# A decoder trunk on one core: pages and PSUM banks as numbered slots, bank turns in the plan, modulation loads at new places

## The chip, the cores and the metric

One core of a Trainium2 chip runs the whole program; the other cores are idle. The metric is the device time of one execution in microseconds (us), the median of three runs. All inputs lie in the chip's memory (HBM) in float32 and the result is written back there.

## The reference, cut to what matters

Two layers on 256 tokens of width 2048. Layer 0 mixes with native sparse attention (NSA: compressed, selected and windowed keys, 16 query heads on 4 key heads), layer 1 with stick-breaking attention; each has a SwiGLU channel mixer of inner width 5632. A vector c gives shift, scale and gate for every norm.

```python
for layer in range(2):
    mod = silu(c) @ mod_w[layer] + mod_b[layer]            # 2048 x 12288, float32
    sh1, sc1, g1, sh2, sc2, g2 = split(mod, 6)
    h = rms_norm(x, g0) * (1 + sc1) + sh1
    if layer == 0:
        y = nsa_mixer(h, ...)                              # w_in 2048 x 5168, w_out 2048 x 2048
    else:
        hk = rms_norm(x, kv_norm_g) * (1 + kv_sc) + kv_sh  # kv_mod_w 2048 x 4096
        k, v = split(hk @ kv_w)                            # 2048 x 4096
        y = stick_breaking(h @ w_q, k, v) @ w_out
    x = x + g1 * rms_norm(y, g1n)
    h = rms_norm(x, g2) * (1 + sc2) + sh2
    gate, up = split(h @ ffn_w_in[layer])                  # 2048 x 11264
    x = x + g2 * rms_norm((silu(gate) * up) @ ffn_w_out[layer], g3)
```

## The kernel before, in words

**Matmuls.** A weight matrix is cut into blocks of 512 rows by 512 columns (1 MB). Each block is fetched into a page of SBUF (a tile of 128 x 2048, 23 pages in all) named raw, and split into two float32r pages: ScalarE copies it rounded (wh), VectorE subtracts (wl = raw - wh). The activations are split the same way. A block meets a half of the tokens (t = 0 or 1) in 12 matmuls of 128x512: high x high, high x low, low x high for four k slices. The results gather in a PSUM bank (acc). Eight banks are shared by these accumulators ("mm") and by all other uses ("x": transposes, scores). In layer 1's channel mixer ("F1") eight of the eleven inner blocks go through a Strassen scheme ("st" units, tiles sacc, rawX, rawY, rawZ, rawW, Sh, Sl, yp), merged between the other units.

**Modulation.** The vectors come from float32 pages of mod_w: 16 loads (modw) for each vector, each followed by one VectorE multiply-add (macc) over 128 x 2048. The first two vectors go by quarters through TensorE (modq, qacc).

**The plan.** The program is written out in full by a planner, `Emit`, while the kernel is built: it keeps a clock for each engine (`clk`), a price for each instruction (`_cost`), and decides from them in which order instructions are put on the engines' queues. `units` is the fixed order of matmul groups on TensorE. `run_bg` advances the epilogues (generators that `yield` until a time). `pump` decides when a block is split and when the next load is put on SP's DMA queue: `LEADS`, `URGENT`, `target` (how many split blocks may wait), `reserve` and `raw_ahead` (pages kept back, loads ahead) are its limits. `order` is the fixed order of all loads; `spread` puts the modw loads among the weight loads, and `AT0` lists places by index in the early part. All queues are in order: what is planned too early waits at the head of its engine's queue, and all behind it waits too.

**Pages and banks.** `pool` gives the planner a sorted list of times at which one of N pages (or banks) comes free; `alloc` takes the earliest, `put` adds a time, `max(self.fin, self.now)`, without saying which tile ends. Which of the N buffers the tile really gets is left to the tile pool of the language (one tag with `bufs=N`). The planner knows accesses to the same cells of a tile; two engines that read different columns of one bank, or the same ones, do not wait for each other in the plan.

**Choices between engines.** `copy`, `scaled` and `affine` take ScalarE or VectorE by comparing the two clocks. In F1, `ep_up` multiplies silu(gate) by up (sg), transposes it on TensorE into a bank (aT), copies the bank on ScalarE (fT) and splits the same bank into the page fa.

**Between the stages** ("transitions": A to F0, F0 to K, B to F1) `residual` runs a serial chain for each half of the tokens: sums of squares (junk, stat), X = X + r z, the next norm's sums, xn, transposes (xT), `affine` (hf) and split (hhF, hhK). While it runs TensorE works on the other half; `emit_lag` lets it run ahead on t = 0 and sets `target` to LAG + LAGX, which is 6.

Of the kernel before, what the change touches and what calls it, by code (L numbers as in the profile page):

```python
# [43 lines left out]
RAW_AHEAD = 7  # L44
SPLIT_AHEAD = 2
SPLIT_MAX = 4
LAG = 5
LAGX = 1
LAGR = 1
TAIL = 6  # L50
AT0 = (22, 36, 50, 60, 61, 62, 62, 63, 64, 67, 68, 69, 70, 70, 72, 72,
       72, 73, 73, 75, 76, 77, 77, 78, 78, 78, 78, 78, 78, 79, 80, 81,
       82, 82, 82, 82, 83, 85, 86, 86, 88, 89, 90, 92, 92, 94, 94, 95)
HEAD = 2
DQ = (0, 2)
T1_LEAD = 2.0
URGENT = (9, 9, 2)
# [3 lines left out]
LEADS = (5.0, 5.0, 5.0)  # L61
M_FFN = 80
PAIRS = (0, 4)
ST_FROM = 3
ST_RAW = 4
ST_RES = 4
ST_TAIL = 1
ST_OVER = 0
M_LAST = 24
M_HEAD = 6  # L70
# [86 lines left out]

class Emit:
# [4 lines left out]
    def __init__(self, nc):  # L163
# [3 lines left out]
        self.readers = {}  # L167
        self.fin = 0.0
        self.bg = []
        self.free = {}  # L170
        self.make = {}
        self.mm = 0
# [33 lines left out]
    def fill(self, aps):  # L206
# [7 lines left out]
        if n > 0:  # L214
            fin = self.fin
            o = self.alloc("x", "idle")
            for _ in range(n):
                self.T.matmul(o[:, 0:2 * P], *self.filler, start=True, stop=True)
            self.free["b"].append(self.clk["PE"])
            self.free["b"].sort()  # L220
            self.fin = fin

    def enter(self, eng, cost, outs, ins, load=0.0):
        t = self.clk[eng] + load
        tr = []
        for ap, w in [(o, True) for o in outs] + [(i, False) for i in ins]:
# [5 lines left out]
            tr.append((c, r, lo, hi, w))  # L232
# [5 lines left out]
            if w:  # L238
                for x in r:
                    if x[0] < hi and lo < x[1]:  # L240
                        t = max(t, x[2] + (0.3 if eng == "DMA" else 0.0))
        lat = 2.3 if eng == "DMA" else 2.5 if eng == "DMA2" else 0.0
        fin = t + cost
        for c, r, lo, hi, w in tr:
# [17 lines left out]
    def pool(self, tag, count, make):  # L262
        self.free[tag] = [0.0] * count
        self.make[tag] = make

    def alloc(self, tag, name, *a):
# [6 lines left out]
        tl = self.make[tag](f"{name}_{self.n}", *a)  # L273
# [24 lines left out]
    def put(self, tag):  # L298
# [3 lines left out]
        f.append(max(self.fin, self.now))  # L302
# [189 lines left out]
def kernel(ctx: ExitStack, tc, consts, x, c, mod_w, mod_b, norm_g, ffn_w_in, ffn_w_out, a_w_in,  # L492
# [10 lines left out]
    E.pool("pg", N_PAGES, lambda name, dt=F32: pp.tile([P, 2048], dt, name=name, tag="pg", bufs=N_PAGES))  # L503
    E.pool("s2", N_S2, lambda name, dt=F32: pp.tile([P, 512], dt, name=name, tag="s2", bufs=N_S2))
    E.pool("sm", 8, lambda name, dt=F32: pp.tile([P, 16], dt, name=name, tag="sm", bufs=8))
    E.pool("b", N_BANKS, lambda name: ps.tile([P, 512], F32, name=name, tag="b", bufs=N_BANKS))
# [36 lines left out]
    def late_consts():  # L543
# [14 lines left out]
        E.put("s2")  # L558
# [23 lines left out]
    E.put("x")  # L582
    E.put("s2")
# [29 lines left out]
    def mac_load(vec, k):  # L613
# [6 lines left out]
        def mac(sl):  # L620
# [7 lines left out]
            if sl.stop == D:  # L628
                E.put("pg")
# [6 lines left out]
    def mod_fin(vec):  # L636
# [6 lines left out]
        E.put("pg")  # L643
# [6 lines left out]
        E.put("s2")  # L650
# [8 lines left out]
        E.put("x")  # L659
# [6 lines left out]
    def macq_load(vec, q, kt):  # L666
# [8 lines left out]
        def add():  # L675
# [9 lines left out]
            E.put("pg")  # L685
# [6 lines left out]
        def mac():  # L692
# [7 lines left out]
            E.put("pg")  # L700
            qcount[vec, q] = n + 1
            if n == len(kts) - 1:
                if q:
# [4 lines left out]
                    E.put("s2")  # L708
# [7 lines left out]
    def macq_half(vec, h, k8):  # L716
# [8 lines left out]
        def mac():  # L725
# [8 lines left out]
            E.put("pg")  # L734
# [6 lines left out]
    def modq_fin(vec, q, h=None):  # L741
# [6 lines left out]
        E.put("x")  # L748
# [4 lines left out]
        E.put("s2")  # L753
# [4 lines left out]
        E.put("x")  # L758
# [3 lines left out]
    def w_load(key, src, nj=4, ncol=NB):  # L762
# [10 lines left out]
        def part(sl):  # L773
# [6 lines left out]
            if sl.stop == sz:  # L780
                E.put("pg")
# [5 lines left out]
    def w_load2(key, src):  # L787
# [13 lines left out]
        def second():  # L801
            V.tensor_tensor(st["l"], st["t"], st["h"].bitcast(F32), op=OP.subtract)
            E.put("pg")
# [8 lines left out]
    ST_FREE = {"P7": 1, "P3": 1, "P4": 2}  # L812
    ST_ORDER = ("P1", "Q5", "P6", "P7", "P3", "P2", "P4")

    def st_load(key):
# [25 lines left out]
        def second():  # L841
            V.tensor_tensor(st["l"], g[ST_OP[nm]], st["h"].bitcast(F32), op=OP.subtract)
            for _ in range(ST_FREE.get(nm, 0)):
                E.put("pg")
# [17 lines left out]

    def copy(out_, in_, scale=1.0):

        if E.clk["ACT"] <= E.clk["DVE"] + (0.1 if in_.space == PSUM else -0.15):
# [6 lines left out]
    def scaled(out_, in_, r):  # L872
        if E.clk["ACT"] <= E.clk["DVE"] - 0.2:
# [4 lines left out]
    def affine(out_, in_, a, b):  # L878
        if E.clk["ACT"] <= E.clk["DVE"] - 0.1:
# [34 lines left out]
    def sumsq(src, acc):  # L914
        j = yield from E.get("s2", "junk")
        A.activation(j, src, AF.Square, accum_out=acc)
        E.put("s2")

    def xT_block(t, kt, r, first=False):
# [6 lines left out]
        yield  # L926
# [3 lines left out]
        E.put("s2")  # L930
# [3 lines left out]
    def h_tile(name, t, kt, r, a, sh, first=False):  # L934
# [12 lines left out]
        E.put("s2")  # L947
# [6 lines left out]
        E.put("x")  # L954
# [12 lines left out]
    def affine_tiles(name, kt, v, a, sh):  # L967

        pg = yield from page_of((name, kt), "h" + name)
        for jj in range(2):  # L970
# [5 lines left out]
            E.put("s2")  # L976

    def h_kept(name, a, sh, deps):
        yield from E.wait(*deps)
        for kt in range(KT):  # L980
# [5 lines left out]
            if kt % 2:  # L986
                E.put("pg")
# [7 lines left out]
    def start_norm():  # L995
# [10 lines left out]
        def normed(kt, t):  # L1006
# [3 lines left out]
            E.put("x")  # L1010
# [4 lines left out]
        for kt in range(KT):  # L1015
# [8 lines left out]
            for jj in range(2):  # L1024
# [7 lines left out]
                E.put("s2")  # L1032
# [3 lines left out]
            if kt % 2 == 1:  # L1036
                E.put("pg")
# [17 lines left out]
    def x_out(key, t, name):  # L1055
# [3 lines left out]
        E.put("pg")  # L1059
# [3 lines left out]
    def gate_rows(key, vec):  # L1063
# [7 lines left out]
        E.put("x")  # L1071
# [3 lines left out]
        E.put("s2")  # L1075
# [6 lines left out]
    def y_block(key, nb, t, acc, part=None):  # L1082
# [9 lines left out]
        if part:  # L1092
            V.tensor_tensor(z, acc, z, op=OP.add)
            E.put("mm")
# [5 lines left out]
        if not part:  # L1100
            E.put("mm")
        E.flag((key, "y", t, nb))

    def residual(key, t, nxt, final=False):
# [25 lines left out]
        E.put("pg")  # L1130
# [952 lines left out]
```

## Time and profile before

| | us |
|---|---|
| median of 3 runs | 2401.85 |
| lowest and highest | 2400.42, 2401.94 |
| the profiled execution's own time | 2399.62 |
| its span (first to last instruction) | 2397.8 |
| granted TensorE clock, mean of the span | 0.995 |

The span is what the views of the trace cover; 1.8 us lie around it. Busy times count an engine's instructions, not its waits. A matmul's end is modelled: of matmuls that follow each other each shows 0.39 us, while they start 0.227 us apart, so idle time that a row shows after a matmul is 0.16 us shorter than the hole between the starts. Nearly all instructions have line 126 (the helper that records them), so groups are told apart by tiles.

### The profile page before, as it was taken

To read this page: it belongs to the slowest core of one execution; us is meant where nothing else is said; L and a number is where in the kernel's file an instruction comes from. 1 tells how busy PE (TensorE), PEld (TensorE's weight loads), DVE (VectorE), ACT (ScalarE), POOL (GpSimd) and SP (SyncE) were. 2 spreads that over 40 slices of the span, in tenths; PEclk is the share of its full clock that TensorE was granted. 3 is DMA by queue.
4 is the path that set the end of the run, shared out by engine and by line. 5 is a ranking of instruction groups with operands and counts; after the bars stand their busy time and mean duration, and the time that the engine had idled before them with its cause. 6 is when DMAs were issued, how large, how long until landed. Compare 5 with 4: busy or idle time off the path is not lost.

```text
span 2397.8 us, 27249 instructions
## 1 busy us (share of the span) xinstructions
PE 2339.1 (98%) x11028; PEld 1890.7 (79%) x11028; DVE 1809.0 (75%) x1493; ACT 1129.3 (47%) x1258; POOL 7.7 (0%) x18
## 2 busy tenths in 40 slices
PE   6999999999999999999999999999999999999998
PEld 4677777877888888888887788887788888888886
DVE  3788788978766667767868787866887788787764
ACT  4343446473333333343455355765445545454443
POOL 0000000000000000000000000000000000000000
PEclk9999999999999999999999999999999999999999
DMA  9997967979887689878758969857965656555581
GB/s 350 389 388 274 354 247 250 360 266 381 288 306 283 225 315 399 327 273 305 283 193 312 371 243 401 324 173 245 362 216 176 217 187 228 175 193 193 175 310 76
DMA packets 266205, 661.74 MB, mean 276 GB/s; under 512 B 12512, under 2 KB 30176, under 8 KB 240224
## 3 DMA queue, kind: packets, MB, share of 16 engines
q1 hardware_dynamic: 263808, 649.13, 74.8%
q0 software_dynamic: 1568, 10.52, 1.1%
q8 instruction: 86, 1.41, 0.3%
q10 hardware_dynamic: 704, 0.36, 0.1%
q14 instruction: 39, 0.32, 0.0%
HBM read 655.74 MB, written 4.23 MB: 275 GB/s over the span
## 4 chain that ended last, share of the span: by engine, by line
PE 69%; issue 22%; DMA 3%; DVE 3%; ACT 2%; SPq 1%; POOL 0%; ACTq 0%; DVEq 0%; POOLq 0%
PE acc L126 57%; PE sacc L126 6%; PE sc L126 1%; PE oT L126 1%; DMA raw<-in_a_w_in_dram 1%; SPq L126 1%; ACT wh L126 1%; DVE wl L126 1%; PE aT L126 1%; DMA modq<-in_mod_w_dram 1%; DMA modw<-in_mod_w_dram 1%; PE pmod L126 0%; PE qacc L126 0%; PE cs L126 0%; ACT junk L126 0%
## 5 line engine op out<-in xcount | busy, mean ns | idle before, releaser
L126 DVE TENSOR_TENSOR wl<-raw,wh 128x2048 fp32r<-128x2048 f32 (+1 forms) x358 | 805.6, 2256 | 281.7 <-ACT wh L126 269.3
L126 ACT ACTIVATE wh<-raw 128x2048 fp32r<-128x2048 f32 (+1 forms) x358 | 671.9, 1886 | 515.0 <-PE acc L126 364.2
L126 PE MATMUL acc<-wh,hhF 128*128 128x512 f32 x2816 | 890.7, 392 | 0.2 <-ACT hhF L126 0.2
L126 PEld LDWEIGHTS acc<-wh,hhF 128*128 128x128 f32 x2816 | 530.8, 189 | 114.9 <-issue 4.2
L126 PE MATMUL acc<-wl,hhF 128*128 128x512 f32 x1408 | 549.7, 390 | 0.0
L126 DVE SCALAR_TENSOR_TENSOR macc<-modw,cact,macc 128x2048 f32<-128x2048 f32 x180 | 422.5, 2347 | 25.9 <-DMA modw<-in_mod_w_dram 16.7
L126 PEld LDWEIGHTS acc<-wl,hhF 128*128 128x128 f32 x1408 | 265.7, 189 | 53.9
L126 PE MATMUL acc<-wh,fa 128*128 128x512 f32 x896 | 278.9, 390 | 0.0
L126 PE MATMUL acc<-wh,hA 128*128 128x512 f32 x640 | 221.5, 405 | 1.4 <-DVE hA L126 0.7
L126 PEld LDWEIGHTS acc<-wh,fa 128*128 128x128 f32 x896 | 168.2, 188 | 35.8 <-issue 0.8
L126 PE MATMUL acc<-wl,fa 128*128 128x512 f32 x448 | 174.3, 389 | 0.0
L126 PE MATMUL acc<-wh,hhK 128*128 128x512 f32 x512 | 161.4, 392 | 0.8 <-ACT wh L126 0.6
L126 PEld LDWEIGHTS acc<-wh,hA 128*128 128x128 f32 x640 | 120.9, 189 | 39.8 <-issue 15.0
L126 PE MATMUL acc<-wl,hA 128*128 128x512 f32 x320 | 126.1, 394 | 3.0 <-DVE wl L126 3.0
L126 ACT ACTIVATE wh<-rawX 128x2048 fp32r<-128x2048 f32 x32 | 61.3, 1916 | 124.4 <-DVE rawX L126 106.4
L126 PEld LDWEIGHTS acc<-wh,hhK 128*128 128x128 f32 x512 | 96.0, 188 | 22.6 <-ACT wh L126 1.1
L126 DVE TENSOR_TENSOR wl<-rawX,wh 128x2048 fp32r<-128x2048 f32 x32 | 73.3, 2290 | 38.7 <-ACT wh L126 38.5
L126 PE MATMUL acc<-wl,hhK 128*128 128x512 f32 x256 | 100.1, 391 | 1.1 <-DVE wl L126 1.0
L126 PEld LDWEIGHTS acc<-wl,fa 128*128 128x128 f32 x448 | 84.1, 188 | 17.2
L126 PE MATMUL acc<-wh,hhB 128*128 128x512 f32 x256 | 87.5, 401 | 0.0
L126 PE MATMUL acc<-wh,oA 128*128 128x512 f32 x256 | 84.9, 398 | 0.0
L126 PE MATMUL acc<-wh,oB 128*128 128x512 f32 x256 | 82.4, 394 | 0.0
(215 smaller groups left out, 2379.4 us busy)
## 6 DMA issues: line engine op xcount, KB each, us to landing
raw<-in_ffn_w_in_dram SPq DMA_DIRECT2D x176, 1024.0 KB, 5.3
modw<-in_mod_w_dram SPq DMA_DIRECT2D x160, 1024.0 KB, 7.4
raw<-in_ffn_w_out_dram SPq DMA_DIRECT2D x56, 1024.0 KB, 6.6
raw<-in_a_w_in_dram SPq DMA_DIRECT2D x40, 1024.0 KB, 14.2
modq<-in_mod_w_dram SPq DMA_DIRECT2D x32, 1024.0 KB, 14.2
modw<-in_kv_mod_w_dram SPq DMA_DIRECT2D x32, 1024.0 KB, 5.7
raw<-in_kv_w_dram SPq DMA_DIRECT2D x32, 1024.0 KB, 7.3
raw<-in_a_w_out_dram SPq DMA_DIRECT2D x16, 1024.0 KB, 7.0
```

The lines of the kernel that those rows point to most:

```text
L126: return f(*a, **k)
```

## The change

- Each page, small tile and bank is a tag of its own with `bufs=1`. `alloc` takes the slot that the plan says is free first and the tile gets exactly that buffer; `put` names the tile, and the slot's time is that of the tile's last planned access (`touch`), not the time at which the generator happens to stand.
- `begin` lets an access of a bank start only after the other engines' accesses of the same bank have ended in the plan. On the chip the waits follow, as before, from what is put where.
- `copy`, `scaled` and `affine` compare the planned ends on the two engines, waits and bank turns included, with a bias each.
- In F1 `ep_up` frees the bank after one copy (fT) and splits from fT; either engine may copy.
- The transposes of sg and xn are put later by set times (LATE, XLATE).
- Constants of the planner: loads ahead 7 to 6 (in the Strassen stretch 4 to 5), pages kept back there 4 to 5, `target` at the transitions 5 + 1 to 6 + 2, `LEADS` and `URGENT` new.
- Places of the modw loads: AT0 new; in F0's part, the head without them goes from 2 blocks to 6 and the tail from 6 to 1; in K, V, Q and O's part from 2 to 8 and from 6 to 11; in F1 sixteen listed places (AT1), four of them late (111 to 129 of 156), instead of the stretch from the 6th to the 24th block. M_FFN goes to 86, but there are 80 such loads, so nothing follows from it.
- SEGS and LASTK replace ST_FROM, ST_TAIL and ST_OVER: for F1 they give the same places of the st units as before (3 to 16, 19 to 32, 35 to 48, 51 to 71). The number of matmuls and of bytes does not change.

```diff
-RAW_AHEAD = 7
+RAW_AHEAD = 6
-LAG = 5
-LAGX = 1
-LAGR = 1
-TAIL = 6
-AT0 = (22, 36, 50, 60, 61, 62, 62, 63, 64, 67, 68, 69, 70, 70, 72, 72,
...
+LAG = 6
+LAGX = 2
+LAGR = 0
+TAIL = 11
+AT0 = (22, 44, 48, 53, 57, 60, 66, 66, 68, 68, 68, 68, 70, 70, 72, 72, 72, 73, 73, 73, 75, 75, 76, 78, 78, 78,
...
-HEAD = 2
+HEAD = 8
-T1_LEAD = 2.0
-URGENT = (9, 9, 2)
+T1_LEAD = 1.0
+URGENT = (9, 8, 1)
-LEADS = (5.0, 5.0, 5.0)
+LEADS = (9.0, 2.0, 9.5)
+HEAD0 = 6
+TAIL0 = 1
-ST_RAW = 4
-ST_RES = 4
-M_LAST = 24
-M_HEAD = 6
+LASTK = (range(6, 11), range(8, 11))
+BIAS = (-0.3, -0.1, -0.2)
+ST_RAW = 5
+ST_RES = 5
+LATE = (0.7, 2.5)
+XLATE = (0.5, 1.1)
+AT1 = (1, 4, 5, 5, 5, 8, 8, 10, 10, 14, 15, 20, 111, 117, 120, 129)
...
+            if ap.space == PSUM:
+                for e, x in self.bank.get(ap.name, {}).items():
+                    if e != eng:
+                        t = max(t, x + LATENCY.get(e, 0.12))
...
+            self.touch[name] = max(self.touch.get(name, 0.0), fin + (lat if w else 1.0 if eng[:3] == "DMA" else 0.0))
+            if eng[:3] != "DMA":
+                self.bank.setdefault(name, {})[eng] = fin
...
-        self.free[tag] = [0.0] * count
+        self.free[tag] = [Free(0.0, i) for i in range(count)]
...
-        tl = self.make[tag](f"{name}_{self.n}", *a)
+        tl = self.make[tag](f"{tag}{t.slot}", f"{name}_{self.n}", *a)
+        self.slot[tl.name] = t.slot
...
-    def put(self, tag):
+    def put(self, tag, tl):
...
-        f.append(max(self.fin, self.now))
+        f.append(Free(max(self.touch[tl.name], self.now), self.slot.pop(tl.name)))
...
-    E.pool("pg", N_PAGES, lambda name, dt=F32: pp.tile([P, 2048], dt, name=name, tag="pg", bufs=N_PAGES))
+    E.pool("pg", N_PAGES, lambda tag, name, dt=F32: pp.tile([P, 2048], dt, name=name, tag=tag, bufs=1))
...
+    def on_act(kind, op, out_, in_, **k):
+
+        return E.ends("ACT", "activation", out_, in_, **k) <= E.ends("DVE", op, out_, in_, **k) + BIAS[kind]
+
     def copy(out_, in_, scale=1.0):
 
-        if E.clk["ACT"] <= E.clk["DVE"] + (0.1 if in_.space == PSUM else -0.15):
+        if on_act(0, "tensor_copy" if scale == 1.0 else "tensor_scalar", out_, in_):
...
-        yield
+        yield E.fin + (0.1 if first is None else XLATE[t])
...
-        yield E.fin + 0.8
+        yield E.fin + LATE[int(key)]
...
+        src = b
         if blk < 2 * PAIRS[int(key)]:
-            L["fT" + key, blk, t] = yield from E.get("s2", "fT")
-            A.activation(L["fT" + key, blk, t], b, AF.Copy)
-        split(pg[:, :, :, t * P:(t + 1) * P], b.rearrange("p (j n) -> p j n", j=4))
-        E.put("x")
+            src = L["fT" + key, blk, t] = yield from E.get("s2", "fT")
+            copy(src, b)
+            E.put("x", b)
+        split(pg[:, :, :, t * P:(t + 1) * P], src.rearrange("p (j n) -> p j n", j=4))
...
-    order += spread(ks, mods_of([(1, 5)]), len(ks) - M_LAST if PAIRS[1] else 20, M_HEAD if PAIRS[1] else HEAD)
+    ms = mods_of([(1, 5)])
+    order += [k for i, key in enumerate(ks) for k in [ms[n] for n, a in enumerate(AT1) if a == i] + [key]]
```

## Rows read from the trace of the kernel before

**Rows 1.** The page's head: busy time of an engine in us, its share of the span, instructions.
```profile
PE 2339.1 (98%) x11028; PEld 1890.7 (79%) x11028; DVE 1809.0 (75%) x1493; ACT 1129.3 (47%) x1258; POOL 7.7 (0%) x18
```

**Rows 2.** Waits of TensorE over the whole span: who waited for whom, us in total, times, longest.
```profile
PE pv L126 <- DMA K<-in_consts_dram: 11.5, 1, 11.5
PE aT L126 <- DVE sg L126: 6.2, 2, 4.0
PE acc L126 <- DVE wl L126: 5.1, 6, 1.8
PE xT L126 <- DVE xn L126: 5.0, 3, 2.2
PE sacc L126 <- DVE wl L126: 4.5, 3, 1.5
PE qacc L126 <- DMA modq<-in_mod_w_dram: 3.6, 6, 1.1
```

**Rows 3.** The chain that ended last, in order of time: start, us, what, how many instructions. One long piece in F0's stretch, and the pieces of TensorE just behind five of its waits.
```profile
598.74 7.00 PE acc L126 x24
...
788.21 132.65 PE acc L126 x585
...
1716.88 4.94 PE acc L126 x12
...
1833.24 2.81 PE sacc L126 x11
...
1962.05 2.79 PE sacc L126 x11
...
2090.85 2.83 PE sacc L126 x11
```

**Rows 4.** Timeline of the start of F1 (1705 to 1720): start, us, engine, instruction, count, and in brackets the engine's idle time before it and what ended that.
```profile
1710.87 3.71 ACT L126 ACTIVATE wh<-raw 128x2048 fp32r<-128x2048 f32 x2 [12.37 <-PE acc L126]
1712.82 2.29 DVE L126 TENSOR_TENSOR wl<-raw,wh 128x2048 fp32r<-128x2048 f32 x1 [1.36 <-ACT wh L126]
1715.03 0.68 DVE L126 TENSOR_TENSOR sg<-sg,acc 128x512 f32<-128x512 f32 x1
1715.77 1.12 PE L126 MATMUL aT<-K,sg 128*128 128x128 f32 x4 [4.03 <-DVE sg L126]
```

**Rows 5.** Stretches with the busy time and instructions of PE, PEld, DVE, ACT and POOL, then the granted TensorE clock, the share of DMA engines and GB/s: the hole of rows 4, what follows it, and what follows the hole at the transition A to F0.
```profile
515.70:520.00 4.30, 4.24 (x20) 3.98 (x21) 2.62 (x7) 2.70 (x8) 0.00 (x0) 0.60 0.02 4
...
1711.70:1715.70 4.00, 0.04 (x1) 0.00 (x0) 2.88 (x3) 2.88 (x2) 0.00 (x0) 0.87 1.05 402
1715.70:1720.50 4.80, 4.73 (x13) 3.89 (x14) 4.80 (x5) 1.08 (x2) 0.00 (x0) 0.50 1.03 399
```

**Rows 6.** Timeline of the early F0 (590 to 600), columns as in rows 4.
```profile
590.87 1.92 ACT L126 ACTIVATE wh<-raw 128x2048 fp32r<-128x2048 f32 x1 [3.29 <-PE acc L126]
...
595.03 2.35 DVE L126 SCALAR_TENSOR_TENSOR macc<-modw,cact,macc 128x2048 f32<-128x2048 f32 x1
...
598.03 0.71 PE L126 MATMUL aT<-K,sg 128*128 128x128 f32 x4 [2.21 <-DVE sg L126]
```

**Rows 7.** Timelines by engine in the Strassen stretch (1808 to 1837), columns as in rows 4.
```profile
1822.84 0.69 DVE L126 CAST fa<-aT 128x512 fp32r<-128x512 f32 x1 [2.35 <-ACT fT L126]
...
1824.77 2.28 DVE L126 TENSOR_TENSOR rawX<-rawX,rawW 128x2048 f32<-128x2048 f32 x1
...
1830.91 2.28 DVE L126 TENSOR_TENSOR wl<-rawX,wh 128x2048 fp32r<-128x2048 f32 x1
...
1833.24 0.50 PE L126 MATMUL sacc<-wl,fa 128*128 128x512 f32 x1 [1.48 <-DVE wl L126]
```

**Rows 8.** Timelines of the three transitions (505 to 520, 1255 to 1272, 1667 to 1680), columns as in rows 4.
```profile
507.90 2.35 DVE L126 TENSOR_TENSOR wl<-raw,wh 128x1024 fp32r<-128x1024 f32 x2
...
515.76 2.89 PE L126 MATMUL xT<-K,xn 128*128 128x128 f32 x16 [2.20 <-DVE xn L126]
...
1265.53 3.12 PE L126 MATMUL idle<-identb 128*128 128x256 bf16 x27
...
1269.52 1.97 PE L126 MATMUL xT<-K,xn 128*128 128x128 f32 x16 [0.86 <-DVE xn L126]
...
1675.63 1.97 PE L126 MATMUL xT<-K,xn 128*128 128x128 f32 x16 [1.97 <-DVE xn L126]
```

**Rows 9.** Timelines by engine in NSA's compression (244 to 258), columns as in rows 4.
```profile
253.75 1.91 ACT L126 ACTIVATE wh<-raw 128x2048 fp32r<-128x2048 f32 x1 [8.78 <-DMA raw<-in_a_w_in_dram]
...
256.37 0.66 PE L126 MATMUL hid<-L,hid 128*128 128x64 f32 x4 [4.31 <-ACT hid L126]
```

**Rows 10.** Stretches, columns as in rows 5: the first 200 us, the rest of NSA, and F0.
```profile
0.00:200.00 200.00, 176.32 (x967) 126.26 (x968) 136.44 (x187) 84.80 (x103) 1.39 (x6) 0.99 0.97 352
200.00:450.00 250.00, 244.77 (x1357) 190.66 (x1357) 212.78 (x306) 122.11 (x261) 1.05 (x2) 0.99 0.84 303
...
604.00:790.00 186.00, 186.00 (x848) 151.90 (x847) 127.60 (x73) 73.43 (x52) 0.00 (x0) 1.00 0.81 288
```

**Rows 11.** The groups of instructions by cost: the multiply-adds of the modulation, their count, busy us and mean ns, idle time before them and what ended it.
```profile
L126 DVE SCALAR_TENSOR_TENSOR macc<-modw,cact,macc 128x2048 f32<-128x2048 f32 x180 | 422.5, 2347 | 25.9 <-DMA modw<-in_mod_w_dram 16.7 <-DMA modw<-in_kv_mod_w_dram 8.4
```

**Rows 12.** DMA issues: what, queue, count, KB each, median us from issue to landing.
```profile
raw<-in_ffn_w_in_dram SPq DMA_DIRECT2D x176, 1024.0 KB, 5.3
```

**Rows 13.** Waits of SP's DMA queue: for whom, us in total, times, longest.
```profile
SPq L126 <- PE acc L126: 811.9, 183, 15.8
```

More of the change, by code (lines that the diff above doesn't have):

```diff
@@ L167, in __init__ @@
         self.readers = {}
+        self.bank = {}
         self.fin = 0.0
@@ L218, in fill, with ends, begin @@
                 self.T.matmul(o[:, 0:2 * P], *self.filler, start=True, stop=True)
-            self.free["b"].append(self.clk["PE"])
-            self.free["b"].sort()
+            self.put("x", o)
             self.fin = fin
-    def enter(self, eng, cost, outs, ins, load=0.0):
+    def ends(self, eng, op, out, in_, **k):
+        return self.begin(eng, [out], [in_])[0] + _cost(eng, op, out, [in_], k, None)
+    def begin(self, eng, outs, ins, load=0.0):
         t = self.clk[eng] + load
@@ L842, in second @@
             V.tensor_tensor(st["l"], g[ST_OP[nm]], st["h"].bitcast(F32), op=OP.subtract)
-            for _ in range(ST_FREE.get(nm, 0)):
-                E.put("pg")
+            for r in ST_FREE.get(nm, ""):
+                E.put("pg", g[r])
             E.ready[key] = (view(st["h"]), view(st["l"]), E.fin)
@@ L1100, in y_block @@
         if not part:
-            E.put("mm")
+            E.put("mm", acc)
         E.flag((key, "y", t, nb))
@@ L1211, in ep_v @@
         V.tensor_tensor(d, acc, part, op=OP.add)
-        E.put("mm")
+        E.put("mm", acc)
         done()
@@ L1447, in nsa_close @@
             yield from E.wait(*[("oA", i, u) for i in range(NG) for u in range(2)])
-            for _ in range(3):
-                E.put("pg")
+            for pg in (kv["ksw"], kv["v"], L0):
+                E.put("pg", pg)
     def nsa_group(g):
@@ L1538, in sb_unit @@
             if all(("oB", i, 0) in E.flags for i in range(NG)):
-                for i in range(4):
-                    E.put("pg")
+                for pg in (kv["kB", 0], kv["kB", 1], kv["vB", 0], kv["vB", 1]):
+                    E.put("pg", pg)
     def sb_group(g):
@@ L1553, in ep_gateff @@
         A.activation(s, acc, AF.Silu)
-        E.put("mm")
+        E.put("mm", acc)
         fst[key, blk, t] = s
@@ L1624, with ep_more @@
     ypart = {}
+    def ep_more(acc, key, nb, t):
+        y = ypart[key, t][:, nb * NB:(nb + 1) * NB]
+        V.tensor_tensor(y, y, acc, op=OP.add)
+        E.put("mm", acc)
+        yield
     def ep_part(acc, key, nb, t):
@@ new lines, in ffn_pairs @@
+        first = True
+        for blocks, sts, out in SEGS[l]:
+            us = in_blocks(blocks)
+            if first:
+                emit_lag(us[:4], LAG)
+                reserve(SPLIT_AHEAD)
+                us = us[4:]
+                first = False
+            if sts:
+                call(lambda: setattr(E, "raw_ahead", ST_RAW))
+                reserve(ST_RES)
+            at = [(a + (b - a) * i / 14.0, u) for p, a, b in sts for i, u in enumerate(st_units(l, key, p))]
+            for i, pair in enumerate(us):
+                while at and at[0][0] < i:
+                    units.append(at.pop(0)[1])
+                units.extend(pair)
+            assert not at
+            if sts:
+                call(lambda: setattr(E, "raw_ahead", RAW_AHEAD))
+                reserve(SPLIT_AHEAD)
+            for nb in range(4) if out else ():
+                emit_plain(mm_units("p" + key, wo, nb * NB, nb, out, fl, lambda a, t, nb_: ep_more(a, key, nb_, t)))
@@ L1849, in cost, with spread @@
         return {"w1": 3.2, "wg": 5.2, "q": 9.0, "qb": 7.3, "st": 2.7}.get(k[0], 5.2)
-    def spread(ks, mods, tail, head=0):
+    def spread(ks, mods, tail, head=0, cost=cost):
         tot = sum(cost(k) for k in ks[head:len(ks) - tail])
@@ L1930, in release @@
         if last_use[u["key"]] == i:
-            del E.ready[u["key"]]
-            E.put("pg")
-            if u["key"][0] != "w1":
-                E.put("pg")
+            for pg in E.ready.pop(u["key"])[:2]:
+                if pg is not None:
+                    E.put("pg", pg)
         if u["kind"] == "mm" and last_lhs[u["lhs"]] == i:
-            E.put("pg")
+            E.put("pg", L[u["lhs"]])
     def weights(key):
```

224 lines of the change are left out of this document (110 added, 114 removed).

## The prediction

> **What bounds the kernel now.** I read the page's head first: TensorE is busy for 98% of the span, VectorE 75%, ScalarE 47% [rows 1]. A busy TensorE is not proof that it is at its peak, so the next view is the chain that ended last, where the reader should look for a long piece without a wait: 585 matmuls of 128x512 in 132.65 us [rows 3], so one each 0.2268 us, and in most of F0 TensorE has no hole at all, 186.00 busy of 186.00 us at clock 1.00 [rows 10]. The change alters the number of matmuls nowhere. Whatever it gains has to come out of the holes, so the third view is TensorE's waits [rows 2], and the fourth the timeline at each hole.
>
> A hole is counted here from the end of the matmul's own 0.227 us, so 0.16 us is added to the idle time of a row after a 128x512 matmul (0.39 shown less 0.23). Behind a hole I also count what the next matmuls take over their steady pace, from the chain.
>
> **Holes by place.**
> - *b, start of F1* [rows 4]: ScalarE stands 12.37 us for pages that TensorE still reads, with two blocks fetched. Its rounding starts at 1710.87, VectorE's subtraction at 1712.82, and the product sg stands behind that in VectorE's queue until 1715.03. TensorE needs the transpose of sg: 4.03 + 0.16 = 4.19 us idle. Behind it the granted clock is 0.50, the lower level, 1.2 GHz, after a stretch in which TensorE did next to nothing [rows 5]; the next 12 matmuls take 4.94 where 12 x 0.2268 = 2.72 is due [rows 3], 2.22 more. Together 6.4.
> - *a, early F0* [rows 6]: the same picture. ScalarE waits 3.29 us for a page, a multiply-add of modulation stands before sg, TensorE idles 2.21 + 0.16 = 2.37, and 24 matmuls take 7.00 in place of 5.44 [rows 3], 1.56 more. Together 3.9.
> - *c, Strassen, three times in the same place* [rows 7]: VectorE's cast of aT waits 2.35 us for ScalarE's fT, a reader of the same bank; then rawX (2.28) and wl (2.28) run late, and TensorE idles 1.48 + 0.16 = 1.64. The next 11 matmuls take 2.81, 2.79 and 2.83 for 2.49 due [rows 3]. Together 3 x 1.64 + 0.95 = 5.9.
> - *d, the three transitions* [rows 8]: xT waits for xn 2.20 + 0.16 = 2.36 and 1.97 + 0.16 = 2.13 us; at F0 to K filler matmuls (idle) hold the place from 1265.53 until the transposes at 1269.52, 3.99. Together 8.5, and 0.40 x 4.30 = 1.7 for the clock of 0.60 behind the first [rows 5].
> - *e, compression* [rows 9]: the small matmul hid waits 4.31 us for ScalarE, which stood 8.78 us with a rounding at the head of its queue until its DMA landed.
> - The start (11.5 us for the constants, 3.6 for modq) and 5.1 us in six waits for wl [rows 2].
>
> **The change part by part.**
> *Slots and true free times.* Removed: the case in which ScalarE, VectorE or SP's queue waits for a page that the plan took for free, with all that is queued behind it. In a and b the wait that starts the chain is of that kind (a page held by TensorE, the two engines otherwise idle); with the plan knowing it, sg goes before the split. Nothing is added; an instruction's semaphore wait exists either way. I take a and b as gone: -3.9 and -6.4. What is late next is the split that was behind: it needs 1.9 + 2.3 us and now starts after sg's 0.68 [rows 4], against 5.44 us of matmuls for each block (24 x 0.2268), so it is hidden while one split block waits in hand; without that cover it costs its 0.68 at most.
> *Bank turns, and fT as the only reader of aT.* In c the 2.35 us wait goes, since the split reads fT; VectorE reaches rawX and wl earlier by about that, which exceeds 1.64: c goes, -5.9. Later transposes (LATE 2.5) add nothing to TensorE: they move behind matmuls that are there anyway, at the price that the bank and sg are held some us longer.
> *Transitions.* The chain from the sums of squares to xn is serial, and nothing shortens it but what no longer stands before it. Before the first one two half subtractions of 2.35 us run on VectorE [rows 8]. Bounds: the whole 8.5 gained, or, with `target` at 8 instead of 6, two more subtractions of 2.29 before each chain, 3 x 4.58 = 13.7 lost. I take a third of the gain, -2.8: 2.35 is nearest to one such instruction moved at one transition, and the other two have less in front.
> *Modulation loads.* Each brings 1 MB on SP's queue and one 2.35 us multiply-add; the 180 take 422.5 us of VectorE [rows 11] before and after. Where they stand in F0, VectorE is busy 127.6 of 186 us beside a TensorE without holes [rows 10], so a move costs nothing there. In NSA DMA engines are busy 0.97 and 0.84 of the time [rows 10] and loads do end waits: bounds are the 3.6 us of modq and 4.3 of e gained, or as much lost. Four late ones in F1 could cost 4 x 2.35 = 9.4 uncovered. I take 0: places in the first 200 us hardly move, and the late four lie where VectorE has room.
> *Fewer loads ahead (6 for 7).* A weight block lands 5.3 us after its issue [rows 12], one block of matmuls; six cover that. Nothing.
> Sum: -3.9 - 6.4 - 5.9 - 2.8 = -19.0. The profiled execution took 2399.62 (span 2397.8 and 1.8 around it), so 2380.6; the median of the runs is 2.2 above it, and 2401.85 - 19.0 gives **2383** for the median.
>
> A rule of the Trainium skill speaks against a part of this. The trace shows three equal holes in c, 128.8 us apart [rows 3]. "Perfetto Trace Analysis", section "Identifying Performance Opportunities", says that the same gap coming again can mean too little SBUF or PSUM for the next tile. By it c, and a and b with it, would be a shortage of pages, which numbering them does not mend; that is the first rival below. The row with the 2.35 us wait for ScalarE [rows 7] speaks for the bank in c.
>
> **The rivals.**
> 1. *Pages are short, not mislaid.* SP's queue waits 811.9 us in total for TensorE to release pages [rows 13], and 23 remain 23, while the plan now keeps up to 8 blocks, 16 pages, ready. Then the splits in a, b and c start no earlier and only d's share comes: 2401.85 - 2.8 = 2399, no difference. Against it: in b ScalarE stood while VectorE ran modulation, so the order of work was free to change.
> 2. *Two more blocks ahead at the transitions.* Place: the three transitions; price: 13.7 us of VectorE before the serial chains, and, as 16 of 23 pages are then held, one landing of 5.3 us late behind each, 15.9. It decides from the point at which these subtractions are planned after the last sums of squares and not into VectorE's idle time ahead of them. 2401.85 - 16.2 + 29.6 = 2415, slower. For it: VectorE is the releaser in all three [rows 8]. Against: the plan's clocks see this queue.
> 3. *All named holes go*: a to e 29.0, the clock's 1.7 and 5.1 of wl [rows 2]: 2401.85 - 35.8 = 2366.
>
> **How the numbers follow.** Forecast (2376 to 2397, with c or a part of d staying) 0.53; rival 1 (2397 to 2402) 0.15; rival 2 (2402 to 2415) 0.15; rival 3 (2366 and below) 0.17. The range of 8 in 10 runs from all holes gone, 2366, into rival 2, 2406. About 0.2%, 4.8 us, can be told from no change, so the borders are 2397.0 and 2406.7: faster holds the forecast, rival 3 and a part of rival 1, 0.74; same most of rival 1 and the milder part of rival 2, 0.14; slower 0.12.
>
> **What would show it.** Right: no wait of TensorE for sg above 1 us at the starts of F0 and F1, no three equal waits of sacc for wl, ScalarE's idle time "PE acc" ahead of wh no longer followed by a hole; granted clock near 1.00 from 1700 to 1725. Transitions: holes before xT of 1 to 2 us still there. Wrong: waits for wl or raw at other places that add up to what a to c gave (rival 1), xT's waits above 4 us (rival 2), or new waits for DMA in NSA, which I priced at nothing.

## The result and the profile after

The changed kernel takes 2378.78 us, the median of 4 runs (2377.19 to 2379.72); the kernel before, run beside it, 2401.32 (2400.42 to 2401.94). The ratio is 0.9906, with a 95% interval of 0.9889 to 0.9923. The profiled execution has a span of 2375.4 us against 2397.8, so 22.4 us are gone, and its mean granted clock is 0.998 against 0.995.

The page's head, which answers to [rows 1]: busy time of an engine in us, share of the span, instructions.

```profile
PE 2329.4 (98%) x11056; PEld 1888.1 (79%) x11056; DVE 1834.6 (77%) x1549; ACT 1107.5 (47%) x1202; POOL 8.5 (0%) x18
```

VectorE has more to do than before (1834.6 against 1809.0) and ScalarE less: a part of the copies out of PSUM went from one to the other. The sum of work was not the gain. The waits of TensorE, answering to [rows 2] (us in total, times, longest):

```profile
PE pv L130 <- DMA K<-in_consts_dram: 14.1, 1, 14.1
PE qacc L130 <- DMA modq<-in_mod_w_dram: 4.2, 4, 1.4
PE acc L130 <- DVE wl L130: 4.0, 4, 1.6
PE pmq L130 <- ACT qrow L130: 3.2, 2, 2.6
PE xT L130 <- DVE xn L130: 2.0, 3, 1.0
PE aT L130 <- DVE sg L130: 1.9, 3, 1.1
PE hid L130 <- ACT hid L130: 1.8, 2, 0.9
```

The wait of sacc for wl is absent. aT's for sg fell from 6.2 to 1.9, and none of it stands at the starts of F0 and F1 (the longest, 1.1, is at 1131 us); xT's for xn fell from 5.0 to 2.0, hid's from 4.3 to 1.8. The long pieces of the chain that ended last, answering to [rows 3] (start, us, what, how many):

```profile
597.44 38.80 PE acc L130 x171
...
1668.43 35.52 PE acc L130 x156
1704.39 2.77 PE acc L130 x12
1707.61 39.46 PE acc L130 x174
...
1812.95 2.72 PE sacc L130 x12
```

Where a block of 12 followed the hole of b with 4.94 us and the holes of c with 2.81 for 11, a block now takes 2.72 to 2.77, the steady pace. The timeline at the start of F1, answering to [rows 4] (in brackets the engine's idle time and what ended it):

```profile
1688.08 1.93 ACT L130 ACTIVATE wh<-raw 128x2048 fp32r<-128x2048 f32 x1 [6.17 <-DMA raw<-in_ffn_w_in_dram]
...
1696.24 2.29 DVE L130 TENSOR_TENSOR wl<-raw,wh 128x2048 fp32r<-128x2048 f32 x1
...
1698.44 2.35 DVE L130 SCALAR_TENSOR_TENSOR macc<-modw,cact,macc 128x2048 f32<-128x2048 f32 x1
1698.50 1.93 ACT L130 ACTIVATE wh<-raw 128x2048 fp32r<-128x2048 f32 x1 [5.85 <-DMA raw<-in_ffn_w_in_dram]
...
1700.70 0.69 DVE L130 TENSOR_TENSOR sg<-sg,acc 128x512 f32<-128x512 f32 x1
```

ScalarE now waits for the raw block to land and no longer 12.37 us for a page that TensorE reads. In VectorE's queue a subtraction and a multiply-add still stand ahead of sg, as before the change, but they no longer run late, and TensorE has no hole. Its stretch (columns as in [rows 5]):

```profile
1698.00:1703.00 5.00, 5.00 (x24) 4.14 (x23) 5.00 (x4) 3.72 (x2) 0.00 (x0) 1.00 1.05 387
```

In the Strassen stretch VectorE makes the sum rawX and the second sg before it turns to a transposed bank. The split reads fT, here copied by VectorE itself, and rawX's wl follows without the wait of 2.35 us that stood in [rows 7] (timeline of VectorE):

```profile
1801.81 2.29 DVE L130 TENSOR_TENSOR rawX<-rawX,rawW 128x2048 f32<-128x2048 f32 x1
1804.01 0.68 DVE L130 TENSOR_TENSOR sg<-sg,acc 128x512 f32<-128x512 f32 x1
1805.64 0.69 DVE L130 COPY fT<-aT 128x512 f32<-128x512 f32 x1 [0.95 <-PE aT L130]
1806.37 0.43 DVE L130 CAST fa<-fT 128x512 fp32r<-128x512 f32 x1
1806.83 0.69 DVE L130 TENSOR_TENSOR fa<-fT,fa 128x512 fp32r<-128x512 f32 x1
1807.44 2.28 DVE L130 TENSOR_TENSOR wl<-rawX,wh 128x2048 fp32r<-128x2048 f32 x1
```

**Where the 22.4 us went.** Both kernels run the same 9120 matmuls of 128x512 into acc and sacc. I number them by their start and take the difference of the starts at the same number; the change of this difference between two numbers is what that stretch gained (-) or lost. The later comparisons of this document, "by progress", are made in the same way.

| stretch (numbers of the matmuls) | us |
|---|---|
| start and NSA (0 to 1200) | -1.7 |
| A to F0 (1200 to 1440) | -3.05 |
| early F0, place a (1440 to 2400) | -3.3 |
| rest of F0 (2400 to 4320) | -0.1 |
| F0 to K (4320 to 4800) | -0.3 |
| K (4800 to 5280) | -1.7 |
| Q and stick-breaking (5280 to 5760) | +0.8 |
| B to F1 (5760 to 6240) | -0.45 |
| start of F1, place b (6240 to 6720) | -8.8, of which 6.9 from 1711 to 1746 us of before |
| three Strassen places c (6720 to 8160) | -1.75, -1.77, -1.82 |
| end (8160 to 9120, and what follows the last matmul) | +1.5 |
| sum | -22.4 |

### The profile page after: what moved, and what is told of

Read it like the earlier page. It is cut to its first block, busy times and chain, and to the rows that moved or that the text cites. A ratio compares the mean times of both kernels' runs of the same rounds, so it can differ in the third digit from the quotient of the medians.

```text
span 2375.4 us, 27243 instructions
## 1 busy us (share of the span) xinstructions
PE 2329.4 (98%) x11056; PEld 1888.1 (79%) x11056; DVE 1834.6 (77%) x1549; ACT 1107.5 (47%) x1202; POOL 8.5 (0%) x18
## 4 chain that ended last, share of the span: by engine, by line
PE 77%; DVE 8%; ACT 4%; DMA 3%; issue 1%; DVEq 0%; SPq 0%; ACTq 0%
PE acc L130 66%; PE sacc L130 6%; DVE wl L130 2%; DVE macc L130 2%; ACT wh L130 2%; DMA modw<-in_mod_w_dram 2%; PE z L130 1%; PE aT L130 1%; ACT junk L130 1%; DMA raw<-in_b_w_q_dram 1%; PE pmod L130 1%; ACT e L130 1%; DVE st L130 1%; DMA raw<-in_a_w_in_dram 1%; PE hT L130 0%
## 5 line engine op out<-in xcount | busy, mean ns | idle before, releaser
L130 PEld LDWEIGHTS acc<-wh,hhK 128*128 128x128 f32 x512 | 96.0, 188 | 21.8 <-ACT wh L130 1.1
```

Of the source, the lines that this page charges most:

```text
L130: return f(*a, **k)
```

## Experiments

Each kernel was timed beside the kernel before on the same chip, whose median was 2400.9 for e1 to e4, 2401.5 for e5 to e8, and 2400.4 for e9 to e12. "Against after" compares with the profiled execution of the changed kernel.

**e1: the numbers of the buffers alone.** The planner, constants and order of before; only the buffer is named.

```diff
 kernel before, with alloc/put/pool of the change, and in put:
-        f.append(max(self.fin, self.now))
+        f.append(Free(max(self.fin, self.now), self.slot.pop(tl.name)))
```

> The old plan with the old constants and the old times at which a page comes free; the one difference from the kernel before is that each page, small tile and bank is handed out by number, the one that the plan holds to be free. The instructions of every engine stand in the same order as before. Theory (holes a and b come from pages that the plan held to be free and that were not): a and b go, 3.3 + 6.9 us by the progress of the matmuls in the changed kernel, so about 2391; c stays, because it is a matter of the bank. Rival (a and b come from the multiply-adds of modulation that stand before sg, and went with their new places): no change, 2401.

2389.86 us (ratio 0.9955, 0.9941 to 0.9970): -11.0. By progress the gain lies in two places, -4.0 from matmul 1440 to 1920 and -6.8 from 6240 to 6720. ScalarE at the start of F1, answering to [rows 4]:

```profile
1693.17 1.92 ACT L131 ACTIVATE wh<-raw 128x2048 fp32r<-128x2048 f32 x1 [1.66 <-DVE macc L131]
1700.02 1.92 ACT L131 ACTIVATE wh<-raw 128x2048 fp32r<-128x2048 f32 x1 [4.93 <-DVE macc L131]
1704.48 1.92 ACT L131 ACTIVATE wh<-raw 128x2048 fp32r<-128x2048 f32 x1 [2.54 <-DVE macc L131]
```

The same instructions stand in the same order on every engine, so sg still follows a subtraction (VectorE):

```profile
1704.36 2.28 DVE L131 TENSOR_TENSOR wl<-raw,wh 128x2048 fp32r<-128x2048 f32 x1
1706.57 0.68 DVE L131 TENSOR_TENSOR sg<-sg,acc 128x512 f32<-128x512 f32 x1
```

But the 12.37 us before the rounding are gone: the page that it gets is one that a multiply-add released, not one that TensorE still reads. So in the plan of before a and b come from the buffer that the pool picked, and neither is a shortage of pages. The waits of TensorE keep the holes of c and the transitions:

```profile
PE xT L131 <- DVE xn L131: 4.8, 3, 2.2
PE sacc L131 <- DVE wl L131: 4.5, 3, 1.5
```

**e2: the change, but the pool of the language picks the buffer.**

```diff
-    E.pool("pg", N_PAGES, lambda tag, name, dt=F32: pp.tile([P, 2048], dt, name=name, tag=tag, bufs=1))
+    E.pool("pg", N_PAGES, lambda tag, name, dt=F32: pp.tile([P, 2048], dt, name=name, tag="pg", bufs=N_PAGES))
 ... the same for s2, sm and b
```

> The changed kernel with the same order of instructions on every engine, but the buffer of each page and bank is picked by the tile pool again. Theory: holes like a and b come back wherever the pool gives a page that TensorE still reads, with ScalarE waiting longer for TensorE: 5 to 12 us slower than the changed kernel, 2384 to 2391. Rival (the gain sits in the order of the instructions and in the places of the loads): no change, 2379.

2387.63 us (0.9946, 0.9931 to 0.9961), 8.9 above the changed kernel. The order of instructions is that of the changed kernel on every engine. The loss comes in small parts: 2.75 in NSA, 1.1 at A to F0, some 2 each in early F0, at F0 to K and in K, and nothing at the start of F1. Among TensorE's waits aT's for sg is larger again, with 1.7 us in early F0 and none at the start of F1:

```profile
PE aT L130 <- DVE sg L130: 4.3, 6, 1.4
```

From both sides, then, the numbering is worth 9 to 11 us, but not at the same places. Hole a comes back by half, hole b not at all: with the new plan b stays away even where the pool picks the buffer.

**e3: the change without the bank turns in the plan.**

```diff
-            if ap.space == PSUM:
-                for e, x in self.bank.get(ap.name, {}).items():
-                    if e != eng:
-                        t = max(t, x + LATENCY.get(e, 0.12))
```

> The changed kernel whose plan knows nothing of bank turns (the loop over the bank's other engines is left out of the plan); all else as changed. Theory: c stays gone, because the split now reads fT and not the bank; the transitions, where ScalarE and VectorE read one bank in turn, lose 1 to 3 us: 2380 to 2383. Rival (bank turns in the plan carry c and the transitions): 8 to 12 us slower, 2387 to 2391.

2388.06 us (0.9944, 0.9929 to 0.9959). My 2380 to 2383 was too low: the turns are worth 9 us. By progress 7.0 are lost in NSA, all of it by 259 us, in the projections and the compression, before the first scores at 262 us. The three transitions lose 0.2, 1.8 and 1.6. The holes of c did not come back, though; no wait of sacc stands among TensorE's.

**e4: all the new code with the constants and places of before.**

```diff
-RAW_AHEAD = 6
-LAG = 6            # and LAGX, LAGR, T1_LEAD, URGENT, LEADS, ST_RAW, ST_RES, LATE, XLATE
-AT0 = (22, 44, ...) # and HEAD, TAIL, HEAD0, TAIL0; F1's last vector by AT1
+RAW_AHEAD = 7
+LAG = 5            # and the others as before
+AT0 = (22, 36, ...) # and the others as before, F1's last vector by spread
```

> The changed kernel with the constants and the places of the modulation loads of the kernel before (loads ahead, LAG, URGENT, LEADS, LATE, XLATE, AT0, HEAD, TAIL, the stretch for the last vector); slots, true free times, bank turns, the choice by ends and fT stay. Theory (the mechanisms carry the gain): a to c stay gone, 2401 - 16 = 2385, and the transitions as before. Rival (the gain hangs on constants that fit the new plan): holes at other places, 2395 to 2402.

2401.95 us (1.0006, 0.9996 to 1.0015): no difference from before. My theory, that the code carries the gain whatever the constants, fell. Against after, NSA is 12.15 us behind by matmul 1200 and A to F0 adds 11.25.

**e5: e1, and the split reads fT.** Either engine may make the copy, and the bank is given back right after it.

```diff
-            A.activation(L["fT" + key, blk, t], b, AF.Copy)
-        split(pg[:, :, :, t * P:(t + 1) * P], b.rearrange("p (j n) -> p j n", j=4))
+            src = L["fT" + key, blk, t] = ...; copy(src, b); E.put("x", b)
+        split(pg[:, :, :, t * P:(t + 1) * P], src.rearrange("p (j n) -> p j n", j=4))
```

> As e1_number_only (old plan, old constants, buffers by number), and in layer 1's channel mixer the split reads fT, with the bank given back after the one copy. Theory (hole c is the wait of VectorE's cast for ScalarE's reading of the same bank): the three waits of sacc for wl go, 3 x 1.8 us, from 2389.9 to 2384. Rival (c comes from the rounding that stands before fT on ScalarE, whoever reads what): the waits stay, 2390.

2385.44 us (0.9931, 0.9916 to 0.9946). By progress against e1 the three places of c gain 1.85, 1.74 and 1.79, 5.4 together, and no wait of sacc for wl is left. The wait of 2.35 us that stood in [rows 7] is not what went. It is still there at all three places; here is the first in VectorE's timeline of e5:

```profile
1816.04 0.43 DVE L131 CAST fa<-fT 128x512 fp32r<-128x512 f32 x1 [2.35 <-ACT fT L131]
...
1820.51 0.68 DVE L131 COPY fT<-aT 128x512 f32<-128x512 f32 x1
```

What went is a second wait, 1.93 us, that the kernel before has a little later. Its second fT stood behind the rounding of rawX in ScalarE's queue, though TensorE had filled the bank by 1826.04 (ScalarE, then VectorE):

```profile
1827.14 1.92 ACT L126 ACTIVATE wh<-rawX 128x2048 fp32r<-128x2048 f32 x1 [4.34 <-DVE rawX L126]
1828.97 0.57 ACT L126 ACTIVATE fT<-aT 128x512 f32<-128x512 f32 x1
...
1829.58 0.69 DVE L126 CAST fa<-aT 128x512 fp32r<-128x512 f32 x1 [1.93 <-ACT fT L126]
```

In e5 VectorE makes this copy itself at 1820.51 and waits for nobody. So the rival had the right place, the rounding ahead of fT, and its waits went all the same, with the copy on the other engine. A split from fT with the second copy left on ScalarE was not run.

The medians differ by 4.4, the profiled executions by 1.0: in that of e5 2.8 were lost in NSA, 0.9 at A to F0 and 0.8 in F0, where e1 and e5 are the same program. Differences of this size by progress, in NSA above all, are therefore not told from chance.

**e6: the change with the split reading the bank again.** e5's edit undone in the changed kernel.

> The changed kernel, but in layer 1's channel mixer ScalarE copies the bank to fT and the split reads the bank again, as before. Theory as for e5: c comes back, 5.5 us, 2384. Rival (a plan that knows bank turns puts the two readers where nothing is late): 2379 to 2381, no wait of sacc.

2382.56 us (0.9920, 0.9904 to 0.9937), 3.8 above the changed kernel. The three equal holes stay away, though VectorE's cast waits 1.93 us for ScalarE's fT again at each of the three places; VectorE has the sum rawX right behind the first sg there, ahead of the second, as in the changed kernel. One hole of 3.0 us appears elsewhere, near 1910, and 1.3 and 1.5 go in NSA and at Q. So with the new constants the holes of c don't need fT to stay away. In the plan of before (e1, e5) e5's edit alone decides over them.

**e7: the change with the old places of all modulation loads.** Of e4's diff the lines with AT0, HEAD, TAIL, HEAD0, TAIL0 and AT1 only.

> The changed kernel with the old places of the modulation loads alone (AT0, HEAD, TAIL, the stretch of the last vector). Theory, formed on e4: the vector for the first transition is ready late, as the 43 filler matmuls there showed, and NSA has its loads at the wrong places: the 10 us in NSA and the 11 us at A to F0 of e4 come from here, so about 2379 + 21 = 2400. Rival (the limits of the planner carry them): 2384 at most.

2390.66 us (0.9957, 0.9943 to 0.9972), between theory and rival: 11.9 lost, in NSA 7.7 by matmul 1200, and 5.7 at A to F0.

**e8: the change with the old limits.** Of e4's diff the lines from RAW_AHEAD to ST_RES only.

> The changed kernel with the planner's old limits alone (loads ahead 7 and 4, pages kept back 4, LAG 5 + 1, LAGR 1, T1_LEAD, URGENT, LEADS). Theory: only the 5.5 us at B to F1 of e4 come from here, 2384 to 2386. Rival (limits and places fit each other, and either one alone is off): 2395 or more, with filler matmuls at a transition.

2412.11 us (1.0046, 1.0031 to 1.0061): 33 lost, slower than before. The rival was right: old limits with old places (e4, 2402) are better than old limits with new places. NSA loses 13.3, A to F0 12.4, Q and stick-breaking 7.6, B to F1 3.2.

**e9: one limit of these.**

```diff
-RAW_AHEAD = 6
+RAW_AHEAD = 7
```

> The changed kernel with one constant put back: RAW_AHEAD 7 in place of 6 (raw weight blocks that may be fetched ahead of their rounding). The forecast priced this term at nothing, since a block lands 5.3 us after its issue and six cover that: by it the time stays within 2376 to 2382 us. Theory after the run with all old limits (2412): there are 23 pages, the plan gives each to a named use, and a raw block more is a page less for the rounded blocks and the modulation, so this single limit carries most of that loss: 2395 to 2412, with filler matmuls above 140 (114 in the changed kernel) and the loss at the same places, NSA from 200 to 450 us, the transition A to F0 and the stick-breaking stretch from 1300 to 1600 us. Rival: the loss belongs to the limits together (modulation ahead, URGENT, LEADS, ST_RAW, ST_RES), each a few us: 2382 to 2390 here.

2407.13 us (1.0027, 1.0017 to 1.0037): 28.4 lost by this number alone, where all the limits lost 33.3. By progress 14.6 are lost in NSA, 11.8 at A to F0 and 6.7 at Q and stick-breaking. What happens at A to F0 is seen in VectorE's timeline of e9, in the step that completes the scale vector (mall) of F0's norm:

```profile
500.04 4.73 DVE L130 SCALAR_TENSOR_TENSOR macc<-modw,cact,macc 128x2048 f32<-128x2048 f32 x2
...
515.08 0.17 DVE L130 TENSOR_TENSOR mall<-pmod,vecT 128x16 f32<-128x16 f32 x1
```

and in that of the changed kernel:

```profile
475.44 2.35 DVE L130 SCALAR_TENSOR_TENSOR macc<-modw,cact,macc 128x2048 f32<-128x2048 f32 x1
...
483.49 0.17 DVE L130 TENSOR_TENSOR mall<-pmod,vecT 128x16 f32<-128x16 f32 x1
```

The vector is complete 31.6 us later, of which 14.6 are the delay of NSA as a whole. In the code `h_all` asks for xn only behind the vector: in e9 the first xn starts at 515.70, right behind mall, in the changed kernel at 494.30, 10.8 us behind it. The serial chain's own last step (stat) ends 3.0 us ahead of this xn in e9 and right ahead of it in the changed kernel, so some 3 us are the vector's by these rows. That the rest of the 11.8 comes from it is not shown. TensorE in e9 around it:

```profile
516.46 2.32 PE L130 MATMUL xT<-K,xn 128*128 128x128 f32 x16 [0.93 <-ACT xn L130]
518.62 4.86 PE L130 MATMUL idle<-identb 128*128 128x256 bf16 x43
523.84 0.50 PE L130 MATMUL acc<-wh,hhF 128*128 128x512 f32 x1 [0.36 <-ACT hhF L130]
```

and in the changed kernel, where the first half's transposes lie between matmuls of the second (acc<-wh,oA) and F0 begins without a gap:

```profile
495.30 0.60 PE L130 MATMUL xT<-K,xn 128*128 128x128 f32 x4
...
496.43 1.47 PE L130 MATMUL xT<-K,xn 128*128 128x128 f32 x12
...
500.27 0.39 PE L130 MATMUL acc<-wh,oA 128*128 128x512 f32 x1
500.49 0.39 PE L130 MATMUL acc<-wh,hhF 128*128 128x512 f32 x1
```

The waits of SP's DMA queue from 380 to 520 us show what the loads stand behind, first in the changed kernel:

```profile
SPq L130 <- PE acc L130: 74.5, 14, 12.2
...
SPq L130 <- DVE macc L130: 15.7, 6, 8.1
```

and in e9:

```profile
SPq L130 <- PE acc L130: 47.5, 13, 8.2
SPq L130 <- DVE macc L130: 37.5, 10, 7.4
```

With one more raw block held, the queue waits less for TensorE's pages and 21.8 us more for pages that the modulation's own multiply-adds still hold. That one page is what modulation lacks is my reading of these rows; a 24th page was not tried. What costs the 14.6 us of NSA is not shown.

The time of mall and what A to F0 lost by progress against after, over all kernels (e1 to e12 by number):

| kernel | mall at, us | lost, matmuls 1200 to 1440 |
|---|---|---|
| after, e11, e10, e6 | 483.5, 484.7, 484.5, 485.1 | 0.0 at most |
| before, e1, e2 | 485.2, 487.5, 487.9 | 3.05, 2.2, 1.1 |
| e5, e3 | 490.4, 490.5 | 3.05, 0.2 |
| e7, e12 | 506.1, 508.0 | 5.7, 12.9 |
| e4, e8, e9 | 511.6, 513.7, 515.1 | 11.25, 12.4, 11.8 |

Up to 491 us the vector is there 12 us before its first use (hf), and the 0 to 3 us have other reasons; from 506 on hf follows within 4 us and 6 to 13 are lost. No run moved the vector alone.

**e10: the old planned delays.** `LATE = (0.8, 0.8)` and `XLATE = (0.1, 0.1)`.

> The changed kernel with the planned delays put back: LATE 0.8 for both layers (0.7 and 2.5 in the change; when the transposes of sg are asked for) and XLATE 0.1 for both (0.5 and 1.1; when the transposes of xn are). Theory: they only choose among matmuls that are there anyway, as the forecast priced them (0): 2377 to 2382, with the transitions' waits of xT for xn as in the changed kernel (1 us at most each) and no wait of sacc. Rival: they are what made the transitions better than the third that was forecast (5.5 us gained against 2.8) and what let the Strassen stretch go without holes: 2383 to 2390, xT's waits back at 2 us each and holes of 1 to 2 us in the stretch from 1746 to 2375 us.

2379.54 us (0.9911, 0.9896 to 0.9925): no difference from the changed kernel, as forecast.

**e11: the old places behind F0 alone.** HEAD 2 and TAIL 6, which are those of K, V, Q and O's part, and `spread` for AT1 in F1. F0's own (HEAD0, TAIL0) stay new here; the expectation counts them to NSA's.

> The changed kernel with the old places of modulation loads in F0 and F1 alone (HEAD 2 and TAIL 6 for 8 and 11; the last vector of F1 spread evenly over the blocks in place of the list AT1); NSA's places (AT0, HEAD0, TAIL0) stay new. Theory: where F0 and F1 have no holes a load's multiply-add lies beside TensorE's work, so these places are worth nothing, as forecast, and the loss of 13.2 us with all old places was NSA's and the transition's: 2376 to 2382. Rival: the four late loads set behind block 110 of F1 and the longer tail of F0 keep VectorE free at F0 to K and B to F1: 2384 to 2390, with holes of 2 us and more at 1234 to 1270 or 1660 to 1720 us.

2377.33 us (0.9902, 0.9887 to 0.9917): no difference either; 1.7 are lost between 1757 and 1815 us and come back between 2144 and 2256. With e7 the places are worth 12 us, all of it that of AT0, HEAD0 and TAIL0 together, and lost in NSA (7.7) and at A to F0 (5.7).

**e12: the new constants and places in the code of before.** The other half of e4: e2's, e3's and e6's edits together, the old `put` time and the old comparison of engine clocks.

> The new constants and places alone, in the code of before: the tile pool picks the buffer, a buffer counts as free from the last planned step, no bank turns in the plan, engine chosen by the old rule, and split reads the bank. Theory, from the run of the opposite half (new code with old constants, 2402, no difference from before): constants and code fit each other and neither half gains alone: 2396 to 2412, with the three sacc waits for wl of about 1.5 us, and waits of aT for sg of 2 to 4 us at the starts of F0 and F1. Rival: the constants were the gain, through NSA's loads and the transitions: 2380 to 2390.

2415.03 us (1.0064, 1.0047 to 1.0081), above the 2412 that I gave as the upper end. The code alone is worth nothing (e4), the constants alone cost 14.6, both together gain 22.5. The three waits of sacc did not come back here, so that part of the theory was wrong: under other limits the same two readers of the bank make no hole, though the cast's wait of 1.93 us for ScalarE's fT is there. Nor did b come back, with the pool picking the buffer: the start of F1 gains 8.8 on the kernel before, as in the changed kernel.

## Why the prediction was right, step by step

- *Holes a and b*, -3.9 and -6.4: they measured -3.3 and -6.9, and -4.0 and -6.8 in e1. The step that names the cause, a page that the plan took for free, is shown by e1 for the plan of before, as nothing else is changed there; the true free times are not needed for it. The step that sg then goes before the split did not happen. In e1 the order is the old one, and in the changed kernel the subtraction of 1696.24 and the multiply-add of 1698.44 still stand ahead of the sg of 1700.70. What went is the wait of the split itself, so whether a split behind sg would be hidden was not put to the test. Nor is the numbering the only way to be rid of b: e2 and e12 do without it and have no hole there.
- *Hole c*, -5.9: -5.3 measured, -5.4 in e5 against e1. The size is right, the reason is not. I had the 2.35 us wait go because the split reads fT; in e5 the split reads fT, that wait stays, and the holes go. What I had not read is the second wait, 1.93 us, for a copy that stood behind a rounding on ScalarE; VectorE making that copy itself takes it away. That two readers of one bank make the hole is thus not shown. In the changed kernel fT is not needed for it: with the new constants the three holes stay away with the bank read twice, with the turns in the plan (e6) and without them (e12). There the sum rawX stands ahead of the second sg in VectorE's queue and not behind it; that this is the reason was not tested alone.
- *Transitions*, -2.8, a third of 8.5: A to F0 -3.05, F0 to K -0.3, B to F1 -0.45, 3.8 together. The 1.7 of K are not the transition's; e1 has 1.5 of them. The size is about right, the reason is not shown. I priced VectorE's subtractions ahead of the serial chain. At A to F0 the kernels with the new constants and an early vector lie within 1.1 us of the changed one, those with the old constants (before, e1, e5) 2.2 to 3.05 behind; which constant does it was not run. Far larger losses there come together with a late modulation vector (506 us and more), which my rows of the transition did not show, since before the change it was there by 485.2 us; of its 11.8 us in e9 some 3 can be read as the vector's.
- *Compression e*, counted in none of the terms: hid's wait fell from 4.3 to 1.8. NSA as a whole gained 1.7, less than e1 and e5 differ there by chance. My bounds from loads in NSA held this.
- *Moved modulation loads*, 0: right behind F0 (e11), wrong ahead of it, where places are worth 12 us beside the new limits (e7). *Fewer loads ahead*, "Nothing": wrong in its reason. A landing of 5.3 us is covered by six and by seven alike; but each raw block holds a page, and in the new plan the seventh costs 28.4 us (e9). In the plan of before seven did not make the vector late (mall at 485.2, and 487.5 in e1). The sum came out because the change turns code, limits and places at once: the code's cost with old constants and the constants' cost with old code are hidden in each other. I had read each as a part with a price of its own, and these parts have none. That my zeros for them did no harm to the sum is luck.
- *Bank turns*, priced within c: 9 us more by e3, 7.0 of it in the first 259 us of NSA, which I had not priced. NSA as a whole gained only 1.7 against before, so this 9 is no gain over before: without the turns the new limits and places lose in NSA (e3).
- *Rival 1*, short pages: wrong for a, b and c. The Trainium skill's rule on the same gap coming again ("Perfetto Trace Analysis", "Identifying Performance Opportunities"), that it can mean too little SBUF or PSUM for the next tile, is not what c shows. With 23 pages and eight banks in both, e5 takes the gaps away; it also gives the bank back one step earlier, but in c the bank was filled by 1826.04 and waited for ScalarE until 1828.97. Pages may be short in NSA, by my reading of e9, where no equal gaps pointed to it. *Rival 2*, subtractions ahead of the chains: xT's waits fell to 1.0 at the most, so it did not happen. *Rival 3* reached 2366; hid, wl and the transitions kept some 10 us of it.
- *The chances*: 0.74 for faster counts in a part of rival 1, but that rival's range begins at the border of 2397; with the ranges as given it is 0.70.

Still open is what in the new code needs the lower limit. With the old constants e5 takes 2385.4 and all the new code (e4) 2402.0; true free times, bank turns in the plan and the choice by planned ends lie between them, and none was put back there alone. So is which of e8's other limits cost the remaining 5 us.

## What to carry to other kernels

Where a planner writes the order of all queues, let it also name the buffer: what it took for free and what the pool handed out differed enough to cost 11 us of 2401 with every instruction in its old place. Read such a wait by who holds the buffer, not by how many there are, and a wait for another engine by what stood ahead in that engine's queue. And do not price constants tuned for one plan singly: undo each half alone before trusting either, and look for a late result with a deadline (here one vector, needed at 496 us) that several limits move together.

## What the runs showed that I had not expected

The same order of instructions on each engine gives times 11 us apart, by the choice of buffer alone (e1). And a lack of real matmuls did not by itself lower the clock: in e9 the 43 fillers hold the place of 4.86 us, about the 4.00 us of the hole b, and the granted clock in and behind them is 1.00, the upper level of 2.4 GHz, where it was 0.50 behind b, in which TensorE stood idle [rows 5]. The stretches of e9:

```profile
518.70:523.70 5.00, 4.78 (x44) 4.04 (x42) 4.86 (x9) 4.97 (x16) 0.00 (x0) 1.00 1.03 390
523.90:528.90 5.00, 4.66 (x20) 3.55 (x21) 4.56 (x10) 2.85 (x9) 0.00 (x0) 1.00 0.80 315
```
